# Distances between matrix inverse, stores and projection, and the split of the key norms, in a fused RWKV-7 and short-convolution block

## Chip, cores and metric

The kernel runs on one core of a Trainium2 chip. Time is the device time of one execution, in microseconds (us). The core has TensorE (PE, matmuls), VectorE (DVE), ScalarE (ACT), GpSimd (POOL) and SyncE (SP), which here issues DMA transfers. PSUM is the memory that PE writes to; SBUF holds everything else that is on the core.

## What is computed

A layer on 512 tokens with 16 learned tokens in front (528 positions, model width 2048): a norm, one wide projection, two groups of heads on its columns, one output projection added to the input, a final norm.

```python
hn = _rmsnorm(h_res, norm_in_g[l])
P = hn @ w_in[l]                      # 528 x 2048 @ 2048 x 8320
Pr, Pc = P[..., :RW_COLS], P[..., RW_COLS:]
...
# group A: RWKV-7, 16 heads of 64
def step(S, inp):
    r_t, w_t, k_t, v_t, kk_t, b_t = inp
    sa = jnp.einsum('bhvk,bhk->bhv', S, kk_t)
    S = (S * w_t[:, :, None, :]
         - sa[..., None] * b_t[:, :, None, :]
         + v_t[..., None] * k_t[:, :, None, :])
    y_t = jnp.einsum('bhvk,bhk->bhv', S, r_t)
    return S, y_t
...
kk = kk / jnp.maximum(jnp.linalg.norm(kk, axis=-1, keepdims=True), 1e-12)
y_a = (yn + bonus) * jax.nn.silu(g_r)
...
# group B: short convolution
y_b = Bg * _causal_depthwise_conv(Cg * hc, conv_w[l]) * jax.nn.silu(g_c)
mix = jnp.concatenate([y_a, y_b], axis=-1)
h_res = h_res + mix @ w_out[l]
```

The recurrence runs in 9 chunks of 64 positions. Within a chunk it needs the inverse of a triangular 64 x 64 matrix for each head, which is built from the products of all keys of the chunk with each other (the Gram matrix).

## The kernel before

**The projection** is the bulk of PE's work: 65 tiles of 128 output columns by all positions. Each weight and each input is split into a high and a low part, and three products are added up (L315): high weights on high input, high on low, low on high. A tile has four quarters of the depth with 24 matmuls each where the positions are in two PSUM halves (258 + 256, or 264 + 264 columns), or 12 where they are one bank of 512 (the tiles B and gc). In a tile with two halves, the halves alternate by depth, so the first half is complete 12 matmuls before the second. SP loads the weights two quarters at a time (L134, `prefetch`, three raw buffers); ACT casts the high part (wh, L126); the low part (wl, L127) is subtracted by DVE for even quarters and by POOL for odd ones. There are six buffers for each part.

The tiles come in a fixed list: low rank, then k, r, v of pairs 0 and 1, g of both, and C, h, B, gc of one convolution tile; then for pairs 2 and 3, 4 and 5, 6 and 7 likewise; then the last four convolution tiles. A "pair" i is two heads. When a tile is complete, L334 takes it out of PSUM (`hh` for tile h, `b` for B, `pr_g` for g), and the convolution (L401 u on POOL, L403 on ACT, L405 on DVE, L413 and L419 the gates) follows behind the tiles h and B; L420 stores its result (`mixd`).

**Other work between projection matmuls.** The projection is a generator. `fill(ns)` takes matmuls out of it, until their estimated cost comes to ns; the numbers stand in the table FW (L43 to 46). PE's order is thus written out by hand: a stage of other work, a fill, the next stage. The orders on DVE, ACT, POOL and SP are made by a list scheduler from priorities and the estimated times.

`later(ns, fn)` puts a transfer on a list with a due time on the projection's clock, ns ahead; `run_pending` issues those that are due, each behind the last weight load on SP's queue. `stash_later` is the same for stores into the scratch array `opd`, from which the recurrence later loads.

**`prepare(i)`**, for each pair: low rank parts, key scalings, the Gram blocks (L631, into `gt`), the key norms and a row sum zb (L655 to 667), copies of the norms to n2 (L670), the transposes bt. The norms are a matmul of 128 x 2 ones against the squares of the keys, in high and low parts; the first 512 positions went into a bank of their own, the last 64 beside the last Gram block. The inverse of the 16 x 16 blocks, y, runs on DVE alone (L706 to 739), in many small links. Stores: y to scratch and back in the layout of 64 x 64 blocks (xT, xo; L745, L746, L754).

**`invert(two)`** for two pairs widens 16 to 64: `fill(solve_first)` for the first two pairs or `fill(solve)` for the others, all pending transfers, then xn (L794, a transpose on DVE, of xT), t (L801, 64 small matmuls, half for each pair), copies ts, z (L815), a predicated copy, and one more level (L825 to 866). At its end stands `fill(out)`, or `fill(begin)` behind the last two pairs.

**`recur`** follows: it loads ct, the operands of a chunk of all pairs (L883, eight loads a chunk), and runs the nine chunks; rz (L902) is the first product of a chunk, zs and zy (L954, L958) come later in it. Then the mixing is split (L1028 to 1042), with `last` and `mix` fills in between, the rest of the projection, and the output projection (L1087).

Of the kernel before, what the change touches and what calls it, by code (L numbers as in the profile page):

```python
# [9 lines left out]
F32 = mybir.dt.float32  # L10
# [8 lines left out]
P = 128  # L19
DM = 2048  # L20
KT = DM // P
SEQ = 512
META = 16
L = SEQ + META
CH = 64
NCH = SEQ // CH + 1
LP = NCH * CH
# [11 lines left out]
O_AR, O_KK, O_BR, O_X, O_V, O_B, O_K = 0, 128, 256, 320, 384, 448, 512  # L39
# [1 line left out]


FW = dict(  # L43
    evac=34, start=1062, lora=2200, gram=8000, gram_b=13500, gram2=5500, misc=2000, v=2000, vt=1000, solve=22500, solve_first=26000,
    tr=3200, lev=3000, cp=4200, out=1500, begin=17000, p=2900, u=2900, s=5200, last=3700, mix=2600,
)


# [28 lines left out]
def hymba_kernel(ctx: ExitStack, tc: tile.TileContext, xt, xtok, w_in, w_out, pv, lup, cst, msk, gf, out):  # L77
    nc = tc.nc
    ctx.enter_context(tc.manual_schedule(engines={mybir.EngineType.PE}))
    cp = ctx.enter_context(tc.tile_pool(name="cp", bufs=1))  # L80
# [16 lines left out]
    def col(off, i=0):  # L97
        return pvt[:, off + i : off + i + 1]
# [56 lines left out]
    pz = ph1.enter_context(tc.tile_pool(name="pz", bufs=2, space=PSUM))  # L155
    pi = ph1.enter_context(tc.tile_pool(name="pi", bufs=1, space=PSUM))
# [5 lines left out]
    def tr(name, dt=F32):  # L162
        return cq.tile([P, LP], dt, tag="tr", name=name, bufs=5)
# [118 lines left out]
    for b in range(2):  # L282
# [5 lines left out]
        out=omm, in0=pvt[:, V_MU : V_MU + 33], scalar1=-1.0, scalar2=1.0, op0=ALU.mult, op1=ALU.add  # L288
    )
    for d, off in (  # L290
# [4 lines left out]
            out=d, in0=pvt[:, off : off + 8], scalar1=0.5, scalar2=None, op0=ALU.mult  # L295
        )
    nc.vector.tensor_scalar(
        out=hv[:, 4], in0=pvt[:, V_KA : V_KA + 8], scalar1=-0.5, scalar2=1.0, op0=ALU.mult, op1=ALU.add
# [183 lines left out]
    def later(ns, fn):  # L482
        pending.append((clock[0] + ns, fn))
        pending.sort(key=lambda e: e[0])
# [30 lines left out]
    def low_rank(i, j, up, w0, name, pad):  # L515
        t = tr(name)
        nc.gpsimd.memset(t[:, META:CH], pad)
        hi, lo = up
        for a, b in ((0, 272), (272, L)):
            z = pz.tile([P, b - a], F32, tag="tz", name=f"{name}_{a}")  # L520
            nc.tensor.matmul(z, hi[:, j], la[:, j, a:b], start=True, stop=False)
            nc.tensor.matmul(z, lo[:, j], la[:, j, a:b], start=False, stop=True)
            with tc.high_priority(offset=AHEAD):
                if a == 0:
                    nc.scalar.activation(t[:, 0:META], z[:, 0:META], AF.Tanh, bias=w0, scale=0.5)
                    nc.scalar.activation(t[:, CH : 5 * CH], z[:, META:272], AF.Tanh, bias=w0, scale=0.5)
                else:
                    nc.scalar.activation(t[:, 5 * CH : LP], z, AF.Tanh, bias=w0, scale=0.5)
            fill(FW["lora"])
        return t  # L530
# [5 lines left out]
    def c3(t):  # L536
        return t.rearrange("p (c s) -> p c s", s=CH)
# [28 lines left out]
    def stash(i, src, o, n, row=0, rows_n=P, c0=0, cn=NCH, step=1):  # L566
        nc.sync.dma_start(spot(i, row, rows_n, c0, cn, step, o, n), src)
# [6 lines left out]
    def stash_later(ns, *a):  # L574
        later(ns, lambda: stash(*a))

    def prepare(i):
        p = i % 2
# [8 lines left out]
        tz = low_rank(i, 0, up, hv[:, 0, i : i + 1], f"tz{i}", -1.0)  # L587
# [12 lines left out]
            out=bk[:, :, 0], in0=c3(k), scalar=hv[:, 2, i : i + 1], in1=c3(te), op0=ALU.mult, op1=ALU.mult  # L600
# [3 lines left out]
            out=ta, in0=ta, scalar1=hv[:, 3, i : i + 1], scalar2=hv[:, 4, i : i + 1], op0=ALU.mult, op1=ALU.add  # L604
        )
        nc.vector.scalar_tensor_tensor(
            out=ar[:, :, 0], in0=c3(k), scalar=col(V_KK, i), in1=e1[:, :, 0:CH], op0=ALU.mult, op1=ALU.mult
# [8 lines left out]
            out=ar[:, 1:NCH, 1], in0=c3(r), in1=e1[:, 1:NCH, 1 : CH + 1], op=ALU.mult  # L616
        )
        nc.vector.scalar_tensor_tensor(
            out=r, in0=r, scalar=hv[:, 5, i : i + 1], in1=ta[:, CH:LP], op0=ALU.mult, op1=ALU.mult
# [8 lines left out]
        gt = cq.tile([P, 2, NCH, P], F32, tag=f"gt{p}", name=f"gt{i}")  # L628
        def gram(z, c, c0):
            for h, hs, ho in heads:  # L630
                nc.tensor.matmul(  # L631
                    z[h][:, c - c0],
                    bk[hs, c, h : h + 2, :].rearrange("p a s -> p (a s)"),
                    ar[hs, c].rearrange("p a s -> p (a s)"),
                    start=True, stop=True,
                )
# [17 lines left out]
        masked(zc, 4, 8)  # L654
        fill(FW["gram2"])  # L655

        ze = [pz.tile([P, P + CH], F32, tag="tz", name=f"g{i}_8_{h}") for h in range(2)]
        gram([z[:, 0:P].unsqueeze(1) for z in ze], 8, 8)
        n2 = tr(f"n2{i}")
        zn = pi.tile([2, SEQ], F32, tag="misc", name=f"n2_{i}")  # L660
        zs = ((zn, 0, SEQ), (ze[0][0:2, P : P + CH], SEQ, LP))
        for z, a, b in zs:
            nc.tensor.matmul(z, ones[:, P : P + 2], sqh[:, a:b], start=True, stop=False)
            nc.tensor.matmul(z, ones[:, P : P + 2], sql[:, a:b], start=False, stop=True)
# [11 lines left out]
        bt = cq.tile([P, NCH - 1, 2, CH // 2, 2], F32, tag="bt", name=f"bt{i}")  # L676
# [5 lines left out]
        sx = scr_x[i % 2]  # L682
# [4 lines left out]
        def blocks(t):  # L687
            return bass.AP(tensor=t.tensor, offset=t.offset, ap=[[BLK, 8 * NCH], [CH, 16], [1, 16]])
# [7 lines left out]
        d = cq.tile([NB, 256], F32, tag="d", name=f"d{i}").rearrange("p (s t) -> p s t", t=16)  # L696
        stash_later(1500, i, ar.rearrange("p c a s -> p c (a s)"), O_AR, 2 * CH)
        for h, hs, ho in heads:
            stash_later(2500 + 1000 * h, i, gt[ho, h], O_KK, 2 * CH, 64 * h, 64)
            stash_later(4500 + 1000 * h, i, gt[hs, h, :, CH:P], O_BR, CH, 64 * h, 64)  # L700
        nd = cq.tile([NB, 16], F32, tag="nd", name=f"nd{i}")
        behind(d, blocks(sg))
        behind(nd, sn.rearrange("(p s) -> p s", s=16))
        y = cq.tile([NB, 256], F32, tag="y", name=f"y{i}").rearrange("p (s t) -> p s t", t=16)
# [14 lines left out]
        for m in (2, 4, 8):  # L719
            for b in range(16 // (2 * m)):  # L720
# [4 lines left out]
                    out=pq,  # L725
# [5 lines left out]
                    out=tq.rearrange("p (i j) -> p i j", i=m), in_=pq, op=ALU.add, axis=AX.X  # L731
                )
                nc.vector.tensor_tensor(
                    out=pq,
# [16 lines left out]
                    ),  # L751
                )

        later(20500 if p else 29000, lambda: nc.sync.dma_start(blocks(sx), y))  # L754
        later(22500 if p else 33000, load_inverse)

        for h, hs, ho in heads:
            for b in range(2):
                for t in range(2):
                    stash_later(  # L760
                        6500 + 1000 * (4 * h + 2 * b + t), i, bt[64 * h + 32 * b : 64 * h + 32 * b + 32, :, t].rearrange("p c s a -> p c (s a)"),
                        O_B + 64 * b, 64, 64 * h + 32 * t, 32, 0, NCH - 1,
                    )
        until("v", i)
        v = got["v", i]
# [244 lines left out]
    for i in range(0, NPAIR, 2):  # L1010
        invert([prepare(i), prepare(i + 1)])
# [56 lines left out]
    last = [[pw.tile([P, 512], F32R, name=f"wlast{a}{j}") for j in range(NL)] for a in range(2)]  # L1068
# [82 lines left out]
    for n in range(4):  # L1151
# [5 lines left out]
        for jj in range(first):  # L1157
# [3 lines left out]
            if n < 2 and jj % 4 == 2:  # L1161
                t, cols = jj // 4, slice(0, 512) if n == 0 else slice(512, DM)
# [11 lines left out]
    with tc.manual_schedule(engines={mybir.EngineType.DVE, mybir.EngineType.Activation, mybir.EngineType.Pool}):  # L1174
# [9 lines left out]
        for part in range(2):  # L1184
# [3 lines left out]
            if part == 0:  # L1188
                finish(2)
                nc.vector.tensor_tensor(  # L1190
                    out=fv[:, 3, 0:1], in0=fv[:, 3, 0:1], in1=ssq[:, 3, 3:4], op=ALU.add
# [60 lines left out]
```

## Time and profile before

| | us |
|---|---|
| median of three runs | 1051.81 |
| lowest and highest | 1050.89, 1053.62 |
| the profiled execution | 1051.02 |
| its span, first to last instruction | 1049.2 |
| mean granted clock of PE | 0.994 |
| DMA moved | 167.48 MB, mean 160 GB/s |

In a row of the timeline the numbers are the start, the duration and, in brackets at the end, how long the engine had been idle and what ended that. `x4` means four instructions put together in a row. In the list of waits the three numbers behind the colon are the total, how many, and the longest. "128x512" is partitions by elements. "issue" is time for which the profile shows no cause. PE's durations overlap, since matmuls are pipelined.

### The profile page before, as it was taken

The numbers are of one execution on the slowest core, as the hardware profiler recorded it, in microseconds if no ns is written. First come the engines' busy times: TensorE is split into PE (matmuls) and PEld (weight loads), VectorE is DVE, ScalarE is ACT, GpSimd is POOL, SyncE is SP. The second block draws the span as 40 slices with busy tenths as digits, with TensorE's granted clock in tenths as the row PEclk, the third lists the DMA queues.
The fourth block names the chain that finished last, engine by engine and source line by source line (L and its number), as shares of the span: only waits on it lengthen the run. The fifth ranks groups of instructions, "written<-read, shape, count | busy, mean of one in ns | idle before, by whom it ended". The sixth has DMA issues, their size and how long they took to land.

```text
span 1049.2 us, 23744 instructions
## 1 busy us (share of the span) xinstructions
PE 1031.6 (98%) x9845; PEld 940.8 (90%) x9845; DVE 580.1 (55%) x1088; ACT 360.0 (34%) x666; POOL 311.1 (30%) x315
## 2 busy tenths in 40 slices
PE   8999998999999999999999999999999999999996
PEld 6999996999998999989999988889898988888885
DVE  6786855569754669753768752444555761212222
ACT  7554313433322434332443232222233342323232
POOL 0132613323222323222323131223233232424132
PEclk8999999999999999999999999999999999999998
DMA  8436565464763273853374748777654958323314
GB/s 292 141 101 166 128 160 145 114 159 103 193 182 114 82 193 84 202 159 114 104 171 103 196 144 291 241 219 221 211 135 150 286 182 296 101 86 95 101 61 161
DMA packets 183404, 167.48 MB, mean 160 GB/s; under 512 B 121472, under 2 KB 143744, under 8 KB 182912
## 3 DMA queue, kind: packets, MB, share of 16 engines
q1 hardware_dynamic: 182720, 164.90, 54.6%
q8 instruction: 77, 1.26, 0.5%
q10 hardware_dynamic: 576, 1.07, 0.3%
q14 instruction: 31, 0.25, 0.1%
HBM read 129.05 MB, written 36.88 MB: 158 GB/s over the span
## 4 chain that ended last, share of the span: by engine, by line
PE 94%; DMA 2%; issue 1%; DVE 1%; POOL 0%; SPq 0%; ACT 0%; DVEq 0%; ACTq 0%; POOLq 0%
PE o L1087 17%; PE ps_v L315 9%; PE ps_g L315 9%; PE ps_k L315 9%; PE ps_gc L315 9%; PE ps_r L315 8%; PE ps_B L315 8%; PE ps_C L315 8%; PE ps_h L315 8%; PE g L631 2%; DMA wq<-in_w_in_dram 1%; PE zs L954 1%; PE zy L958 1%; PE ps_lora L315 1%; PE rz L902 1%
## 5 line engine op out<-in xcount | busy, mean ns | idle before, releaser
L127 POOL TENSOR_TENSOR wl<-wr,wh 128x512 fp32r<-128x512 f32 x150 | 208.8, 1392 | 460.0 <-ACT wh L126 439.6
L126 ACT CAST wh<-wr 128x512 fp32r<-128x512 f32 x312 | 190.0, 618 | 411.7 <-PE o L1087 93.0
L127 DVE TENSOR_TENSOR wl<-wr,wh 128x512 fp32r<-128x512 f32 x162 | 121.7, 756 | 224.4 <-ACT wh L126 223.2
L1087 PE MATMUL o<-wh,m 128*128 128x512 f32 (+1 forms) x484 | 145.2, 384 | 0.0
L1087 PEld LDWEIGHTS o<-wh,m 128*128 128x128 f32 x484 | 89.6, 188 | 21.3
L1087 PE MATMUL o<-wl,m 128*128 128x512 f32 (+1 forms) x242 | 92.6, 389 | 0.0
L315 PE MATMUL ps_h<-xh,wh 128*128 128x258 f32 (+1 forms) x256 | 72.7, 284 | 0.6 <-issue 0.6
L315 PE MATMUL ps_k<-xh,wh 128*128 128x264 f32 x256 | 73.2, 286 | 0.0
L315 PE MATMUL ps_v<-xh,wh 128*128 128x264 f32 x256 | 73.2, 286 | 0.0
L315 PE MATMUL ps_k<-xl,wh 128*128 128x264 f32 x256 | 73.1, 285 | 0.0
L315 PE MATMUL ps_k<-xh,wl 128*128 128x264 f32 x256 | 72.9, 285 | 0.0
L315 PE MATMUL ps_r<-xh,wh 128*128 128x258 f32 (+1 forms) x256 | 72.2, 282 | 0.7 <-ACT wh L225 0.7
L315 PE MATMUL ps_v<-xh,wl 128*128 128x264 f32 x256 | 72.7, 284 | 0.0
L315 PE MATMUL ps_v<-xl,wh 128*128 128x264 f32 x256 | 72.7, 284 | 0.0
L315 PE MATMUL ps_C<-xh,wh 128*128 128x258 f32 (+1 forms) x256 | 72.5, 283 | 0.0
L315 PE MATMUL ps_g<-xl,wh 128*128 128x258 f32 (+1 forms) x256 | 72.4, 283 | 0.0
L315 PE MATMUL ps_h<-xl,wh 128*128 128x258 f32 (+1 forms) x256 | 72.3, 283 | 0.0
L315 PE MATMUL ps_C<-xl,wh 128*128 128x258 f32 (+1 forms) x256 | 72.3, 282 | 0.0
L315 PE MATMUL ps_r<-xh,wl 128*128 128x258 f32 (+1 forms) x256 | 72.1, 282 | 0.0
L315 PE MATMUL ps_r<-xl,wh 128*128 128x258 f32 (+1 forms) x256 | 72.0, 281 | 0.0
L315 PE MATMUL ps_g<-xh,wh 128*128 128x258 f32 (+1 forms) x256 | 71.9, 281 | 0.0
L315 PE MATMUL ps_C<-xh,wl 128*128 128x258 f32 (+1 forms) x256 | 71.9, 281 | 0.0
(274 smaller groups left out, 2715.9 us busy)
## 6 DMA issues: line engine op xcount, KB each, us to landing
wr<-in_w_in_dram SPq DMA_DIRECT2D x127, 512.0 KB
ct<-opd SPq DMA_DIRECT2D x64, 288.0 KB
wr<-in_w_out_dram SPq DMA_DIRECT2D x32, 512.0 KB
opd<-ar SPq DMA_DIRECT2D x8, 576.0 KB
opd<-gt SPq DMA_DIRECT2D x16, 288.0 KB
opd<-bt SPq DMA_DIRECT2D x64, 64.0 KB
xres<-in_xtok_dram SPq DMA_DIRECT2D x4, 768.0 KB
out_dram<-xres SPq DMA_DIRECT2D x6, 512.0 KB
```

The source lines that it names most:

```text
L126: nc.scalar.copy(hi, rq)
L127: eng.tensor_tensor(out=lo, in0=rq, in1=hi.bitcast(F32), op=ALU.subtract)
L315: nc.tensor.matmul(ps[r], ww[:, w], xx[:, kt, a:b], start=(kt == 0 and n == 0), stop=(kt == KT - 1 and n == 2))
L631: nc.tensor.matmul(z[h][:, c - c0], bk[hs, c, h : h + 2, :].rearrange("p a s -> p (a s)"), ar[hs, c].rearrange("p a s -> p (a s)"), start= ...
L902: nc.tensor.matmul(z[e][ho if e else hs, 0, k], t[hs, o : o + CH], t[hs, O_V : O_V + CH] if part else st[hs, 4 * e + k], start=(part == 0 ...
L954: nc.tensor.matmul(d[hs, j], w, x[hs], start=(a == 0), stop=(a == b - 1))
L958: nc.tensor.matmul(d[ho, j], t[hs, o : o + CH], x[hs], start=(a == 0), stop=(a == b - 1))
L1087: nc.tensor.matmul(ps[t + p], mm[:, tk], ww[:, o], start=(jj == 0 and q == 0), stop=(jj == KT - 1 and q == 2))
```

## The change

Three things, all in the table and in `prepare`. The fills in front of the inverses grow: solve from 22500 to 24500, solve_first from 26000 to 30000, and begin, between the last inverse and the recurrence, from 17000 to 19500. The key norms are taken in two parts of 288 positions instead of 512 and 64; the second still lies beside the last Gram block, whose tile becomes wider for the first head and narrower for the second. And due times move: the Gram blocks' stores by 3000 ns each, bt's eight stores from 6500 + 1000 n to 9000 + 900 n, and, for pair 1 alone, the store of y and the load of xT and xo by 2000 ns.

```diff
 FW = dict(
-    evac=34, start=1062, lora=2200, gram=8000, gram_b=13500, gram2=5500, misc=2000, v=2000, vt=1000, solve=22500, solve_first=26000,
-    tr=3200, lev=3000, cp=4200, out=1500, begin=17000, p=2900, u=2900, s=5200, last=3700, mix=2600,
+    evac=34, start=1062, lora=2200, gram=8000, gram_b=13500, gram2=5500, misc=2000, v=2000, vt=1000, solve=24500, solve_first=30000,
+    tr=3200, lev=3000, cp=4200, out=1500, begin=19500, p=2900, u=2900, s=5200, last=3700, mix=2600,
 )
...
-        ze = [pz.tile([P, P + CH], F32, tag="tz", name=f"g{i}_8_{h}") for h in range(2)]
+        ze = [pz.tile([P, P + 288 * (1 - h)], F32, tag="tz", name=f"g{i}_8_{h}") for h in range(2)]
         gram([z[:, 0:P].unsqueeze(1) for z in ze], 8, 8)
         n2 = tr(f"n2{i}")
-        zn = pi.tile([2, SEQ], F32, tag="misc", name=f"n2_{i}")
-        zs = ((zn, 0, SEQ), (ze[0][0:2, P : P + CH], SEQ, LP))
+        zn = pi.tile([2, 288], F32, tag="misc", name=f"n2_{i}")
+        zs = ((zn, 0, 288), (ze[0][0:2, P : P + 288], 288, LP))
         for z, a, b in zs:
             nc.tensor.matmul(z, ones[:, P : P + 2], sqh[:, a:b], start=True, stop=False)
             nc.tensor.matmul(z, ones[:, P : P + 2], sql[:, a:b], start=False, stop=True)
...
         for h, hs, ho in heads:
-            stash_later(2500 + 1000 * h, i, gt[ho, h], O_KK, 2 * CH, 64 * h, 64)
-            stash_later(4500 + 1000 * h, i, gt[hs, h, :, CH:P], O_BR, CH, 64 * h, 64)
+            stash_later(5500 + 1000 * h, i, gt[ho, h], O_KK, 2 * CH, 64 * h, 64)
+            stash_later(7500 + 1000 * h, i, gt[hs, h, :, CH:P], O_BR, CH, 64 * h, 64)
...
-        later(20500 if p else 29000, lambda: nc.sync.dma_start(blocks(sx), y))
-        later(22500 if p else 33000, load_inverse)
+        later((22500 if i == 1 else 20500) if p else 29000, lambda: nc.sync.dma_start(blocks(sx), y))
+        later((24500 if i == 1 else 22500) if p else 33000, load_inverse)
...
-                        6500 + 1000 * (4 * h + 2 * b + t), i, bt[64 * h + 32 * b : 64 * h + 32 * b + 32, :, t].rearrange("p c s a -> p c (s a)"),
+                        9000 + 900 * (4 * h + 2 * b + t), i, bt[64 * h + 32 * b : 64 * h + 32 * b + 32, :, t].rearrange("p c s a -> p c (s a)"),
```

## The prediction

> **What bounds the kernel now.** I read the page's busy line and its chain of work first, then the list of what PE waited for, then windows and timelines around each wait.
>
> ```profile
> PE 1031.6 (98%) x9845; PEld 940.8 (90%) x9845; DVE 580.1 (55%) x1088; ACT 360.0 (34%) x666; POOL 311.1 (30%) x315
> ...
> PE 94%; DMA 2%; issue 1%; DVE 1%; POOL 0%; SPq 0%; ACT 0%; DVEq 0%; ACTq 0%; POOLq 0%
> ...
> PE ps_B L315 <- DVE wl L127: 1.6, 1, 1.6
> ...
> PE ps_gc L315 <- DVE wl L127: 0.9, 1, 0.9
> PE ps_h L315 <- issue: 0.6, 1, 0.6
> PE t L801 <- DVE xn L794: 0.5, 1, 0.5
> PE rz L902 <- DMA ct<-opd: 0.5, 1, 0.5
> PE zy L958 <- issue: 0.2, 1, 0.2
> ...
> 791.90:861.80 69.90, 69.90 (x407) 61.47 (x406) 46.75 (x63) 25.81 (x44) 24.67 (x18) 1.00 0.72 215
> ```
>
> TensorE (PE) is busy 98% of the span and carries 94% of the chain, so time can change in two ways only: matmuls that become cheaper or dearer, and moments at which PE stands still. Behind the arrow is what ended a wait, then total, number, longest (us). The six rows are all the waits inside the body: 1.6+0.9+0.6+0.5+0.5+0.2 = 4.3 us. The rest of PE's idle time lies in the first 22 us and the last 10, which the change doesn't touch. A change that does not shorten matmuls can win 4.3 us at most (0.4%), while what it can lose is open. The last row (window, PE busy and count, the other engines, clock, DMA share, GB/s) is the stretch of pure projection behind the recurrence: from here the generator takes what the kernel wants earlier.
>
> **Part 1: key norms in two halves.**
>
> ```profile
> 84.52 0.40 PE L663 MATMUL n<-sq_h,ones 128*2 128x512 f32 x1
> ...
> 84.98 0.19 PE L663 MATMUL g<-sq_h,ones 128*2 128x64 f32 x1
> ...
> 85.04 0.48 PE L666 MATMUL zb<-rk_h,ones 128*128 128x512 f32 x1
> 85.36 0.40 PE L667 MATMUL zb<-rk_l,ones 128*128 128x512 f32 x1
> 85.59 0.28 PE L315 MATMUL ps_r<-xl,wh 128*128 128x258 f32 x1
> ...
> 302.77 0.28 PE L315 MATMUL ps_h<-xl,wh 128*128 128x256 f32 x1
> ...
> 303.59 0.28 PE L315 MATMUL ps_h<-xh,wl 128*128 128x256 f32 x1
> ```
>
> The first columns are start and duration; durations overlap in the pipeline, so a matmul costs the distance to the next start. From 84.52 to 85.59 the group takes 1.07 us: 2 x 0.23 for 512 columns, 0.06 for the two of 64, and then 0.32 + 0.23 for zb. The first zb costs 0.09 more than its kind: its 128-column weights don't disappear behind a 64-column matmul. A 256-column one costs (303.59 - 302.77)/7 = 0.117, so 288 columns cost 0.117 + (32/256) x (0.23 - 0.117) = 0.131 (estimate). After: 4 x 0.131 + 2 x 0.23 = 0.99, so 0.08 less, times 8 groups = 0.7 us. Bounds: 0 (the 0.09 stays) and 0.8. The two copies to n2 change from 512 + 64 columns to 288 + 288, the same sum, on ACT, which is busy 34%.
>
> **Part 2: the first inverse (solve_first 26000 to 30000).** Three of the six waits stand here.
>
> ```profile
> 150.82 0.43 DVE L334 TENSOR_TENSOR hh<-ps_h,rs 128x258 f32<-128x258 f32 x1 [3.09 <-PE ps_h L315]
> ...
> 153.09 0.41 DVE L334 TENSOR_TENSOR hh<-ps_h,rs 128x256 f32<-128x256 f32 x1
> 153.42 1.16 DVE L733 TENSOR_TENSOR prod<-y,tt 72x512 f32<-72x512 f32 x1
> ...
> 157.67 1.54 POOL L127 TENSOR_TENSOR wl<-wr,wh 128x512 fp32r<-128x512 f32 x1 [1.92 <-ACT wh L126]
> ...
> 158.00 1.76 DVE L127 TENSOR_TENSOR wl<-wr,wh 128x512 fp32r<-128x512 f32 x1
> ...
> 159.81 0.50 PE L315 MATMUL ps_B<-xh,wl 128*128 128x512 f32 x1 [1.59 <-DVE wl L127]
> ...
> 168.12 0.70 DVE L794 STREAM_TRANSPOSE xn<-xT 128x512 f32<-128x512 f32 x1
> ...
> 168.88 0.69 PE L801 MATMUL t<-xn,gt 64*64 64x64 f32 x32 [0.50 <-DVE xn L794]
> ```
>
> DVE works in program order. At 150.82 it had stood 3.09 us before the first half of hh, with the last links of the 16x16 inverse (L739, L724, L730, L733) queued behind it. All but L733 and the last L739 then run in front of the second half at 153.09, and from there leads a chain: u on POOL, the convolution on ACT and DVE, wl at 158.00, PE at 159.81. In the changed program's order L739, L724 and L730 come ahead of the first hh, in that 3.09 us hole; only L733 (1.16 us at 153.42) is left between the halves. The second half then waits for its own matmuls: its last is 12 matmuls (12 x 0.117 = 1.4) behind that of the first half (150.82 - 0.32 + 1.4 = 151.9), so it runs at about 152.2 instead of 153.09. The chain moves up by 0.9, and the 1.59 shrinks to about 0.7.
>
> The wait at 168.88 goes: L801 comes 18 matmuls of 512 columns later (18 x 0.23 = 4.1 us) with xn behind a load that moves about 1 us only (one weight load now stands ahead of the stored y on SP's queue). The 0.92 of ps_gc stays: the product b still stands on DVE ahead of the split it waits for. Gain 0.9 + 0.5 = 1.4 us; bounds 0 and 1.59 + 0.92 + 0.50 = 3.0.
>
> The Trainium skill ("SBUF — State Buffer", section "Who interferes with whom") says that a DVE instruction with two inputs in SBUF contends with a GpSimd instruction that reads SBUF, and that who issues first decides who waits. The trace agrees: wl at 158.00 took 1.76 us, until just after POOL's wl ended at 157.67 + 1.54 = 159.21. By that rule the ps_B wait would go altogether (0.7 us more gain) if DVE's split were issued first; both follow ACT's casts, which move together, so I keep POOL first.
>
> **Part 3: the later inverses (solve 22500 to 24500), three pairs.** None of them waits today.
>
> ```profile
> 282.98 0.43 DVE L334 TENSOR_TENSOR pr_g<-ps_g,rs 128x258 f32<-128x258 f32 x1 [2.14 <-PE ps_g L315]
> 283.33 0.15 DVE L733 TENSOR_TENSOR prod<-y,tt 72x8 f32<-72x8 f32 x1
> ...
> 298.92 0.63 SPq L746 DMA_DIRECT2D xo<-sx  x1
> ...
> 302.23 0.69 DVE L127 TENSOR_TENSOR wl<-wr,wh 128x512 fp32r<-128x512 f32 x1 [4.01 <-ACT wh L126]
> 302.84 0.70 DVE L794 STREAM_TRANSPOSE xn<-xT 128x512 f32<-128x512 f32 x1
> ...
> 303.80 1.16 PE L801 MATMUL t<-xn,gt 64*64 64x64 f32 x64
> 304.89 0.39 PE L315 MATMUL ps_h<-xh,wh 128*128 128x256 f32 x1
> ...
> 308.07 0.28 PE L315 MATMUL ps_h<-xh,wl 128*128 128x256 f32 x1
> ...
> 308.39 0.42 DVE L334 TENSOR_TENSOR hh<-ps_h,rs 128x256 f32<-128x256 f32 x1 [0.74 <-PE ps_h L315]
> ```
>
> L801 moves 18 matmuls back within the h tile, and so passes the end of the tile's first half: that half's last matmul is the 15th behind the old place of t, and t now comes three later. The scheduler answers on DVE: the evacuation hh of that half, which stood behind xn, now stands in front of wl and of the xn of the pair's second member. Before, DVE's order was wl 302.23, xn 302.84 and hh after t. Now xn cannot start before PE has finished a matmul that is only three ahead of the one that needs xn.
>
> By rows: that 15th matmul starts at 303.59 + 15 x 0.117 = 305.35 (t no longer in between). An hh follows the start of its last matmul by about 0.32 (308.39 after 308.07), so 305.67. To the next instruction 0.35 (282.98 to 283.33), wl to xn 0.61, xn 0.70: it ends at 307.33, PE goes on at 307.39 (0.06 as at 168.82 to 168.88). PE would want t's second half at 303.59 + 18 x 0.117 + 0.21 + 0.47 = 306.4 (0.21 is the step into t, 0.5 its first half, of the 1.09 from 303.80 to 304.89). Lost: 1.0 us per pair. The orders of pairs 4/5 and 6/7 show the same, so 3.0 us. Lower bound 0.6 each (hh at once), upper 2.2 (restart 0.1, and a wl drawn out as at 158.00, 1.1): 1.8 to 6.5. I take 3.0, the value that the rows of this place give without either extra.
>
> The stall delays nothing but PE. The loads behind it: y's chain of the second member, whose first links ran ahead of pr_g at 282.98, now starts behind it; as DVE stood idle for 2.14 us there, it ends about 2 us later; the last of its four loads is issued at some 301 instead of 298.92 and, with the 3.9 us at most that the load took before (298.92 to 302.84), is in by 304.9, ahead of 306.6.
>
> **Part 4: begin 17000 to 19500, and the stores.**
>
> ```profile
> 632.55 2.92 SPq L883 DMA_DIRECT2D ct<-opd  x6
> 639.08 0.32 SPq L420 DMA_DIRECT2D mixd<-cv  x1
> 639.50 5.64 SPq L883 DMA_DIRECT2D ct<-opd  x10
> ...
> 644.78 0.33 PE L902 MATMUL rz<-ct 64*64 64x64 f32 x4 [0.48 <-DMA ct<-opd]
> ...
> 632.00:636.00 4.00, 4.00 (x20) 3.30 (x19) 0.81 (x2) 0.92 (x2) 0.14 (x1) 1.00 0.68 171
> 636.00:640.00 4.00, 4.00 (x36) 4.00 (x35) 2.94 (x4) 1.58 (x3) 1.30 (x1) 1.00 1.01 382
> ```
>
> The recurrence's first rz comes 41 matmuls later (2000 + 2500 ns of projection; 41 x 0.117 = 4.8 us): at 649.1 instead of 644.3 for its last four. On SP, the store of the convolution at 639.08 used to stand between the sixth and seventh of the eight loads ct; now it stands in front of seven of them. 256 KB and 7 x 288 KB at 382 KB/us take 5.9 us. After the issue at 632.55 the window to 636 carried under half of the next one's 382 GB/s, so data flow some 2 to 3 us after the issue: 639.1 + 3 + 5.9 = 648.0. So the 0.48 wait goes; bounds a gain of 0.5 and a loss of 0.6 (begin's own delay not sufficient by one load, 0.75). I take 0.4. The moved stores of Gram blocks and bt are the same transfers at the same size, some 3 us of projection later; what reads them is this recurrence, after 632. Their issues on SP cost nothing while SP keeps ahead of the weight loads. The projection taken earlier, 4 + 3 x 2 + 2.5 = 12.5 us, is missing from the 69.9 us of pure projection at 791.9. The mixing steps there spread over 4 x 3.7 + 8 x 2.6 = 35.6, and 57.4 remain: cost nothing; without that cover the mixing would add what is missing.
>
> **Sum.** -0.7 - 1.4 - 0.4 + 3.0 = +0.5 us on the profiled execution's 1051.0: 1051.5. The median of the three runs, 1051.8, lies 0.8 above the profiled one, so 1052.3 in the median's terms.
>
> **The rivals.** A measurement can tell 0.3% (3.2 us) from no change: under 1048.7 is faster, over 1055.0 slower.
>
> *Faster: hh doesn't hold xn.* If the hh waits in pairs 1 to 3 cost nothing, 2.5 us of gains remain: 1049.3. If the other rows of the first pair (0.7 of ps_B, 0.92 of ps_gc) and the issue rows (0.6, 0.2) go too, 1046.9. For it: the shift in the first pair also moves every weight split after it, so any of these can vanish. Against it: DVE's order is fixed in the program, and 150.82 shows DVE standing 3.09 us for such an hh with ready work behind.
>
> *Slower: the xT loads come late.* In pairs 1 to 3 the y chain ends about 2 us later while the store of y and the loads keep their place on the projection's clock. If SP stands at the store and the loads land after 306.6 instead of 304.9, each us beyond adds 1 us per pair. It decides beyond 1.7 us of delay; at 2.7 us it makes 3 us, 1055.3, at 3.7 us 1058. For it: SP is one queue, on which the store of y holds up all that follows. Against it: before, 3.9 us was the whole way from issue to use.
>
> *No effect.* Positions move, but waits move along with them, as splits are ordered by the same projection clock: only the norms' 0.7 us: 1051.1.
>
> **How the numbers follow.** Forecast 0.40 (its own range 1050.5 to 1054.5), faster 0.24, slower 0.26, no effect 0.10. Of the faster case some three quarters lie below 1048.7 (0.18), of the slower one most above 1055.0, and a little of the forecast's upper bound (6.5 us lost) too: 0.27. The rest, 0.55, is within. Leaving out a tenth at each end gives 1047.8 to 1056.5.
>
> **What would show it.** Right: a list of PE's waits with three new rows t from xn of about 1.0 us each, near 306, 457 and 608, each with an hh directly ahead of wl and xn on DVE; the t row of the first pair gone; ps_B's 1.6 down to about 0.7; the norm group 0.99 long with four 288-column matmuls; rz's row gone. Wrong: no t rows (then faster), a t row ended by xT's load or over 2 us long (then slower), a wait on weight splits that is new, or PE's busy sum changed by more than 1 us.

## The result, and the profile after

| | before | changed |
|---|---|---|
| median of 22 runs each, us | 1051.82 | 1050.01 |
| lowest to highest | 1048.86 to 1053.90 | 1047.15 to 1051.71 |
| profiled execution, its span | 1051.02, 1049.2 | 1049.89, 1048.1 |

The ratio is 0.9982, with a 95% interval of 0.9975 to 0.9989: 1.8 us faster, between 1.2 and 2.6. The forecast was 1052.3, slower by half a us. The time lies within the wide range of 1047.8 to 1056.5 and within the 0.3% called no change, but below the forecast's own range of 1050.5 to 1054.5, and the sign was wrong.

The busy line of the page and PE's waits in the changed kernel (line, what ended the wait, then total, number, longest in us):

```profile
PE 1030.6 (98%) x9845; PEld 940.2 (90%) x9845; DVE 577.1 (55%) x1088; ACT 359.7 (34%) x666; POOL 302.2 (29%) x315
```

```profile
PE t L801 <- DVE xn L794: 2.3, 3, 0.8
...
PE ps_gc L315 <- DVE wl L127: 0.9, 1, 0.9
...
PE rz L902 <- DMA ct<-opd: 0.6, 2, 0.4
...
PE ps_h L315 <- issue: 0.3, 1, 0.3
PE rz L954 <- issue: 0.3, 1, 0.3
```

The three new waits of t are there, the old one is gone, ps_gc is the same to a tenth. ps_B is gone altogether, where 0.7 was forecast; rz is still there. PE's busy time is 1.0 us less with the same 9845 matmuls.

The first norm group in PE's timeline of the changed kernel (start, duration, instruction):

```profile
84.03 0.29 PE L663 MATMUL n<-sq_h,ones 128*2 128x288 f32 x1
84.16 0.29 PE L664 MATMUL n<-sq_l,ones 128*2 128x288 f32 x1
84.29 0.30 PE L663 MATMUL g<-sq_h,ones 128*2 128x288 f32 x1
84.42 0.30 PE L664 MATMUL g<-sq_l,ones 128*2 128x288 f32 x1
84.55 0.39 PE L666 MATMUL zb<-rk_h,ones 128*128 128x512 f32 x1
84.78 0.40 PE L667 MATMUL zb<-rk_l,ones 128*128 128x512 f32 x1
85.02 0.28 PE L315 MATMUL ps_r<-xl,wh 128*128 128x258 f32 x1
```

84.03 to 85.02 is 0.99 us, as worked out, with 0.13 for 288 columns and 0.23 for the first zb instead of 0.32. The load of its weights now starts 0.13 us before it (84.42); in the kernel before it started 0.03 before (85.01), behind a 64-column matmul.

DVE's timeline in the first pair, and POOL's at the same place:

```profile
150.14 0.43 DVE L334 TENSOR_TENSOR hh<-ps_h,rs 128x258 f32<-128x258 f32 x1 [1.19 <-PE ps_h L315]
150.48 1.14 DVE L733 TENSOR_TENSOR prod<-y,tt 72x512 f32<-72x512 f32 x1
151.54 0.42 DVE L334 TENSOR_TENSOR hh<-ps_h,rs 128x256 f32<-128x256 f32 x1
151.88 0.67 DVE L739 TENSOR_REDUCE y<-prod 72x64 f32<-72x512 f32 x1
...
155.58 1.79 DVE L127 TENSOR_TENSOR wl<-wr,wh 128x512 fp32r<-128x512 f32 x1
```

```profile
152.04 1.29 POOL L401 TENSOR_TENSOR u<-u,hh 128x514 f32<-128x514 f32 x1 [9.90 <-DVE hh L334]
```

From the first hh to the second are 1.40 us instead of 2.27. And u on POOL takes 1.29 us where it took 2.17, as POOL's row of the kernel before shows:

```profile
153.58 2.17 POOL L401 TENSOR_TENSOR u<-u,hh 128x514 f32<-128x514 f32 x1 [10.80 <-DVE hh L334]
```

There u began just after the start of DVE's L733 (153.42 to 154.58), which reads two tiles in SBUF, and ended 1.17 us after that; here L733 is issued before the second hh and u begins behind both. Of the other seven u of the kernel before, six take 1.28 to 1.31 us. The one at 797.84 took 1.76, beside DVE's L994 (796.66 to 798.42, also with two inputs in SBUF), and ended 1.18 us after that. L739, which reads one tile and runs beside u here (151.88), doesn't lengthen it.

PE and DVE around t in pair 3:

```profile
302.58 0.69 PE L801 MATMUL t<-xn,gt 64*64 64x64 f32 x32
304.04 0.70 PE L801 MATMUL t<-xn,gt 64*64 64x64 f32 x32 [0.76 <-DVE xn L794]
304.66 0.39 PE L315 MATMUL ps_h<-xh,wh 128*128 128x256 f32 x1
```

```profile
302.34 0.43 DVE L334 TENSOR_TENSOR hh<-ps_h,rs 128x258 f32<-128x258 f32 x1 [6.47 <-PE ps_h L315]
302.68 0.68 DVE L127 TENSOR_TENSOR wl<-wr,wh 128x512 fp32r<-128x512 f32 x1
303.28 0.70 DVE L794 STREAM_TRANSPOSE xn<-xT 128x512 f32<-128x512 f32 x1
```

DVE stands idle for 6.47 us until the end of the h half, then hh, wl and xn follow in one chain, and PE goes on 0.06 after xn ends. The rows in the other two places, at 455.85 and 607.66, are the same: 0.76 each. It is the step of part 3, in the order it gave.

SP's queue ahead of the recurrence, and what PE waits for there:

```profile
631.70 0.44 SPq L883 DMA_DIRECT2D ct<-opd  x1
638.19 0.33 SPq L420 DMA_DIRECT2D mixd<-cv  x1
638.62 10.41 SPq L883 DMA_DIRECT2D ct<-opd  x15
```

```profile
648.00 0.33 PE L902 MATMUL rz<-ct 64*64 64x64 f32 x4 [0.17 <-DMA ct<-opd]
648.74 0.33 PE L902 MATMUL rz<-ct 64*64 64x64 f32 x4 [0.41 <-DMA ct<-opd]
```

Seven loads stand behind the store, as foreseen, and PE goes on from the last that rz waits for 10.5 us after the store's issue, where 8.9 was worked out.

**A stretch to compare by.** Executions differ ahead of everything that the change touches. So I take, for the kernels below, the stretch from the first norm matmul (L663) to the first matmul of the output projection (L1087), each read from the list of a line's instructions (after the colon the least, median and greatest ns, then first and last start):

```profile
L663 PE MATMUL n<-sq_h,ones x8: 291/295/295, 84.0 to 569.6; 128*2 128x288 f32 x8
...
L1087 PE MATMUL o<-wh,m x484: 278/393/402, 860.5 to 1023.0; 128*128 128x512 f32 x148, 128*128 128x256 f32 x14
```

That is 776.5 us. Before it is 861.6 - 84.5 = 777.1.

### The profile page after: what moved, and what is told of

It reads as the page before. It is cut to its first block, busy times and chain, and to the rows that moved or that the text cites. A ratio compares the mean times of both kernels' runs of the same rounds, so it can differ in the third digit from the quotient of the medians.

```text
span 1048.1 us, 23743 instructions
## 1 busy us (share of the span) xinstructions
PE 1030.6 (98%) x9845; PEld 940.2 (90%) x9845; DVE 577.1 (55%) x1088; ACT 359.7 (34%) x666; POOL 302.2 (29%) x315
## 4 chain that ended last, share of the span: by engine, by line
PE 92%; DMA 4%; DVE 2%; SPq 1%; issue 1%; ACT 0%; POOL 0%; DVEq 0%; ACTq 0%
PE o L1087 17%; PE ps_v L315 9%; PE ps_gc L315 9%; PE ps_k L315 9%; PE ps_g L315 9%; PE ps_r L315 8%; PE ps_B L315 8%; PE ps_C L315 7%; PE ps_h L315 7%; PE g L631 2%; PE zs L954 1%; PE ps_lora L315 1%; PE zy L958 1%; DMA gated<-g 1%; PE rz L902 1%; DVE wl L127 1%
## 5 line engine op out<-in xcount | busy, mean ns | idle before, releaser
L127 POOL TENSOR_TENSOR wl<-wr,wh 128x512 fp32r<-128x512 f32 x150 | 204.4, 1363 | 466.0 <-ACT wh L126 450.4
L1087 PE MATMUL o<-wh,m 128*128 128x512 f32 (+1 forms) x484 | 145.4, 384 | 0.0
L1087 PEld LDWEIGHTS o<-wh,m 128*128 128x128 f32 x484 | 89.6, 188 | 21.3
L1087 PE MATMUL o<-wl,m 128*128 128x512 f32 (+1 forms) x242 | 92.7, 390 | 0.0
L315 PE MATMUL ps_h<-xh,wl 128*128 128x258 f32 (+1 forms) x256 | 72.3, 282 | 0.0
```

The lines of the kernel that those rows point to most:

```text
L127: eng.tensor_tensor(out=lo, in0=rq, in1=hi.bitcast(F32), op=ALU.subtract)
L315: nc.tensor.matmul(ps[r], ww[:, w], xx[:, kt, a:b], start=(kt == 0 and n == 0), stop=(kt == KT - 1 and n == 2))
L1087: nc.tensor.matmul(ps[t + p], mm[:, tk], ww[:, o], start=(jj == 0 and q == 0), stop=(jj == KT - 1 and q == 2))
```

## The experiments

Ratios are to the kernel before, run beside each, with 95% intervals. "Stretch" is the one above, in one profile of each.

| kernel | median, us | ratio | stretch | ps_B | t from xn | rz from ct |
|---|---|---|---|---|---|---|
| before, again | 1051.93 | 1.0002 (0.9990 to 1.0014) | 777.8 | 1.6 | 0.5 | 1.2 |
| changed, again | 1049.52 | 0.9983 (0.9974 to 0.9992) | 776.2 | none | 3 x 0.76 | 0.4 |
| norms alone | 1050.01 | 0.9985 (0.9974 to 0.9995) | 776.5 | 0.6 | 0.5 | 1.0 |
| stores alone | 1052.18 | 1.0007 (0.9995 to 1.0020) | 778.0 | 1.6 | 0.8 | 0.7 |
| norms and stores | 1049.29 | 0.9985 (0.9972 to 0.9997) | 774.9 | none | 0.5 | 0.7 |
| solve_first and pair 1's due times | 1050.00 | 0.9991 (0.9982 to 1.0001) | 776.3 | 1.6 | none | 0.9 |
| begin alone | 1049.76 | 0.9986 (0.9977 to 0.9994) | 776.1 | 1.6 | 0.5 | none |
| solve alone | 1054.84 | 1.0028 (1.0016 to 1.0040) | 780.7 | 1.6 | 2.8 | 0.8 |
| changed, solve 22500 | 1046.86 | 0.9955 (0.9942 to 0.9967) | 773.1 | none | none | none |
| changed, solve 24000 | 1047.01 | 0.9952 (0.9938 to 0.9965) | 773.1 | none | none | none |
| changed, solve 25500 | 1073.88 | 1.0207 (1.0192 to 1.0221) | 798.6 | none | 17.6 | none |

A shorter stretch, from the first norm matmul to the one of the third pair's group, holds only the first of the inverses (84.52 to 223.91 before, 84.03 to 220.75 with the change). It repeats to 0.05 us between two profiles of one kernel, so it can tell the parts apart:

| kernel | first to third norm group, us | against before |
|---|---|---|
| before, twice | 139.39, 139.41 | |
| stores alone | 139.38 | 0.0 |
| solve_first and pair 1's due times | 138.67 | -0.7 |
| norms alone | 138.24 | -1.2 |
| norms and stores | 137.55 | -1.85 |
| changed, twice | 136.72, 136.77 | -2.65 |

**Both kernels again.** No edit.

> The kernel before, unchanged, for a second profile. The waits theory (what the change does is the sum of PE's waits and the norms' matmuls, the same in every execution): the waits ps_B from wl about 1.6, ps_gc 0.9, t from xn 0.5 stand again, within 0.1 us; time equal to before. Rival (waits vary between executions, and the first profile of before showed fewer than usual): some wait in the body is longer by 0.5 us or more, or one is new.

> The changed kernel, unchanged, for a second profile. Waits theory: three waits of t from xn of 0.76 us each, ps_gc 0.9, no ps_B, as in its first profile; about 1.8 us under before. Rival (waits vary): these differ by 0.3 us or more from the first profile, above all rz from ct, which ends with a load.

Waits that end with DVE are the same to a tenth from one execution to the next. The one that ends with a load is not: rz waited 0.48 and 1.20 us before, 0.58 and 0.41 with the change. So the 0.5 which the prediction started from was the low one of two. The first norm matmul started at 84.5 and 84.3, and 84.0 and 85.7: an execution's time scatters by over a us from the start alone.

**The norms alone.**

```diff
-zn = pi.tile([2, SEQ], F32, tag="misc", name=f"n2_{i}")
-zs = ((zn, 0, SEQ), (ze[0][0:2, P : P + CH], SEQ, LP))
+zn = pi.tile([2, 288], F32, tag="misc", name=f"n2_{i}")
+zs = ((zn, 0, 288), (ze[0][0:2, P : P + 288], 288, LP))
```

> The key norms' part alone: 288 + 288. By the prediction's part 1: 0.7 us of matmuls, 1051.1, and the waits of before. Theory of a reordered DVE: the shorter norm group alone makes the scheduler put the last links of the 16x16 inverse ahead of the first hh, so u on POOL runs 1.3 instead of 2.2 us and the ps_B wait falls from 1.6 to between 0 and 0.6, though solve_first is as before: 1049.9 to 1050.5. t from xn stays at 0.5.

DVE and POOL of this kernel in the first pair:

```profile
150.33 0.43 DVE L334 TENSOR_TENSOR hh<-ps_h,rs 128x258 f32<-128x258 f32 x1 [1.47 <-PE ps_h L315]
150.67 1.14 DVE L733 TENSOR_TENSOR prod<-y,tt 72x512 f32<-72x512 f32 x1
151.85 0.68 DVE L739 TENSOR_REDUCE y<-prod 72x64 f32<-72x512 f32 x1
152.45 0.41 DVE L334 TENSOR_TENSOR hh<-ps_h,rs 128x256 f32<-128x256 f32 x1
```

```profile
152.94 1.30 POOL L401 TENSOR_TENSOR u<-u,hh 128x514 f32<-128x514 f32 x1 [10.64 <-DVE hh L334]
```

Without any longer fill, links of the 16x16 inverse have moved ahead of hh. Between the two hh it is still 2.12 us, nearly the 2.27 of before; but u runs in 1.30 instead of 2.17. The 0.15 and the 0.87 are the 1.0 that ps_B lost of its 1.6 us. An edit of four matmuls on PE and the two copies behind them, in groups of which the first stands at 84 us, changed the list scheduler's order on DVE at 150. Which of these pieces it reacted to is not shown.

**The stores, and the norms with the stores.**

```diff
-stash_later(2500 + 1000 * h, ...)
-stash_later(4500 + 1000 * h, ...)
+stash_later(5500 + 1000 * h, ...)
+stash_later(7500 + 1000 * h, ...)
...
-6500 + 1000 * (4 * h + 2 * b + t)
+9000 + 900 * (4 * h + 2 * b + t)
```

> The later due times of the Gram blocks' and bt's stores alone. By the prediction's part 4 they cost and bring nothing: the time of before, ps_B 1.6, ps_gc 0.9, t from xn 0.5. Rival (the stores make room for the loads that rz waits for, or for weights): a wait in the body shrinks by 0.5 us or more, and the time by as much.

> Norms 288 + 288 and the later stores, no fill changed. Theory that the gain at ps_B is DVE's order alone: here the order is hh, L733, hh, L739 as in the changed kernel (with the norms alone L739 also stands ahead of the second hh, and 0.6 of the 1.6 us was left), so ps_B goes to 0 without any longer fill; ps_gc 0.9 and t from xn 0.5 stay. 1.6 + 0.1 restart + 0.65 of matmuls = 2.3 us under before. Rival (solve_first takes the last 0.6): ps_B about 0.6, 1.7 us under before.

The later stores alone change nothing in the first inverse, and the ratio can't be told from 1. They have one small cost: at 303.43 DVE's xn waits 1.22 us for the load of xT, and t 0.30 behind it, which is the second wait in the 0.8 of the table. Together with the norms they move one more instruction: L739 goes behind the second hh, and ps_B is gone without solve_first. The waits of that kernel:

```profile
PE ps_gc L315 <- DVE wl L127: 0.9, 1, 0.9
...
PE rz L902 <- DMA ct<-opd: 0.7, 2, 0.4
PE ps_h L315 <- issue: 0.6, 1, 0.6
PE t L801 <- DVE xn L794: 0.5, 1, 0.5
```

The stretch fell by 2.5 us against the mean of the two before (777.45), near the 2.3 expected; the ratio, 1.6 us with an interval from 0.3 to 2.9, agrees and doesn't tell it from the rival's 1.7. What does is that ps_B's row is gone, and the 0.7 us between the norms' 138.24 and 137.55 in the shorter stretch.

**solve_first.**

```diff
-solve_first=26000
+solve_first=30000
...
-later(20500 if p else 29000, ...)
-later(22500 if p else 33000, load_inverse)
+later((22500 if i == 1 else 20500) if p else 29000, ...)
+later((24500 if i == 1 else 22500) if p else 33000, load_inverse)
```

> solve_first 30000 alone, with pair 1's store and load 2000 ns later; the norms stay 512 + 64. By the prediction's part 2 (the longer fill moves the chain of the 16x16 inverse): ps_B falls from 1.6 to about 0.7 and t from xn goes, 1.4 us gained. Theory that the norms' edit reordered DVE: here DVE's order around hh is that of before, so ps_B stays at 1.6, and only t from xn (0.5 and 0.1 for the restart) goes: about 0.6 us gained.

```profile
PE ps_B L315 <- DVE wl L127: 1.6, 1, 1.6
...
PE ps_gc L315 <- DVE wl L127: 0.9, 1, 0.9
PE rz L902 <- DMA ct<-opd: 0.9, 2, 0.5
```

ps_B stays whole, and the t row is gone. The interval of the ratio reaches 1; the shorter stretch is 0.7 us less. So the longer first fill is worth the 0.5 us of xn and a restart, and nothing of the rest that the prediction put under its name.

**begin.**

```diff
-begin=17000
+begin=19500
```

> begin 19500 alone. By the prediction's part 4 the wait of rz from ct (0.5 and 1.2 us in two profiles of before) shrinks, by 0.4 us or more; the other waits stay. Rival (the store of the convolution holds the loads back as far as rz moves): rz waits 0.5 or more still.

rz does not wait any more, and the kernel is 1.5 us faster (0.6 to 2.4). Here, as before, six loads stand ahead of the store of the convolution; in the changed kernel it is one (the SP rows above), and rz waits in both its profiles. With the change and solve at 22500 or 24000 it is six and three, and rz doesn't wait. That fits a gain of begin which is partly given back by the order on SP; no kernel here moves that store alone.

**solve: alone, taken back, and at two other lengths.**

```diff
-solve=22500
+solve=24500     # alone, in the kernel before
...
-solve=24500     # in the changed kernel
+solve=22500     # and 24000, and 25500
```

> solve 24500 alone. Theory of hh in front of xn: three waits t from xn of 0.76 us, each with a restart of 0.1: 2.6 us more than before, about 1054.4, with the waits of before beside them. Rival (the longer solve gains by giving the loads time): 1051.8 or less.

> The changed kernel with solve back at 22500, all else as changed. Theory that the longer solve costs by hh in front of xn: the three waits of t from xn (0.76 each and 0.1 for each restart) go, all else stays as in the changed kernel: 2.6 us less, about 1047.4, under both kernels. Rival (the longer solve is what brought the gain): time back to about 1051.

> The changed kernel with solve at 24000 instead of 24500: t moves by about 5 matmuls less, and on DVE xn of the second member stands in front of hh again. Theory of hh in front of xn: what costs is the place on DVE, not the length, so the three waits are gone and the time is that of solve 22500, 1046.9. Rival (the wait grows with the length of the fill): three quarters of the cost remain, 0.57 per pair, about 1049.

> The changed kernel with solve at 25500: now both halves of hh and the convolution's first DVE instruction (L405) stand in front of xn on DVE. Theory of hh in front of xn: xn waits behind hh, u on POOL (1.3), ACT (0.7) and L405 (1.0), about 4.2 us per pair, so 12.6 us over solve 22500: about 1059.5. Rival (the wait was loads that come late, and a longer fill gives them time): t waits less than 0.76, at most 1050.

Alone, the longer solve costs 2.9 us (1.7 to 4.2), and taken out of the changed kernel it gives 3.2 us by the medians (2.7 against the changed kernel run beside it) and 3.2 by the stretch. At 24000 nothing is lost: DVE of that kernel has xn ahead of hh again.

```profile
302.35 0.71 DVE L794 STREAM_TRANSPOSE xn<-xT 128x512 f32<-128x512 f32 x1 [1.13 <-DMA xT<-sx]
304.83 0.43 DVE L334 TENSOR_TENSOR hh<-ps_h,rs 128x258 f32<-128x258 f32 x1 [1.77 <-PE ps_h L315]
```

So it isn't the length: 1500 ns more cost nothing, and 2000 cost three us, since between them t passes the end of the h half. At 25500 both hh, and the convolution's DVE step that waits for POOL and ACT, stand ahead of xn; DVE's rows and PE's:

```profile
302.62 0.43 DVE L334 TENSOR_TENSOR hh<-ps_h,rs 128x258 f32<-128x258 f32 x1 [6.47 <-PE ps_h L315]
304.02 0.42 DVE L334 TENSOR_TENSOR hh<-ps_h,rs 128x256 f32<-128x256 f32 x1 [0.97 <-PE ps_h L315]
306.58 1.54 DVE L405 SCALAR_TENSOR_TENSOR cv<-u,pvt,cv 128x512 f32<-128x512 f32 x2 [2.13 <-ACT cv L403]
308.04 1.75 DVE L127 TENSOR_TENSOR wl<-wr,wh 128x512 fp32r<-128x512 f32 x1
309.71 0.70 DVE L794 STREAM_TRANSPOSE xn<-xT 128x512 f32<-128x512 f32 x1
```

```profile
310.47 1.13 PE L801 MATMUL t<-xn,gt 64*64 64x64 f32 x32 [5.85 <-DVE xn L794]
311.53 0.79 PE L315 MATMUL ps_B<-xh,wh 128*128 128x512 f32 x1
312.12 0.63 PE L315 MATMUL ps_B<-xl,wh 128*128 128x512 f32 x1
312.55 0.63 PE L315 MATMUL ps_B<-xh,wl 128*128 128x512 f32 x1
```

The chain is the one expected, hh, u, L403, L405, wl, xn. PE waits 5.85 us for it instead of 4.2: both of the convolution's DVE steps run (1.54 for two, not 1.0 for one) and wl takes 1.75. The wait is not all that it costs: PE's clock falls, in the last column but two of the windows:

```profile
310.00:316.00 6.00, 5.53 (x43) 4.46 (x44) 1.10 (x2) 2.11 (x4) 1.27 (x1) 0.51 0.31 90
316.00:330.00 14.00, 14.00 (x181) 11.05 (x180) 6.69 (x13) 4.22 (x9) 4.01 (x5) 1.00 0.33 97
```

After the 5.85 us of idleness PE runs at 0.51 until about 316, with matmuls of 512 columns 0.43 us apart instead of 0.23. What that costs shows from the first matmul of tile h to the last of gc, the same 450 matmuls in each kernel. In the three places this takes 46.29, 45.23 and 46.15 us, against 38.75, 38.75 and 38.76 in the changed kernel (and 37.83 or 37.84 with solve 24000). Of the 7.5, 6.5 and 7.4 us more, 5.1 each are the longer wait; 2.4, 1.4 and 2.3 are left for the slow clock. These 21.4 us are most of the 22.2 by which the stretch grew; the medians differ by 23.9, and the rest is not accounted for.

The Trainium skill ("TensorE: Matmul & The Clock Gate", section "What's actually happening") says that an idle window of about 3.4 us halves the clock. The runs agree on both sides of it: 5.85 us did, 1.59 us did not, as the window around it in the kernel before shows:

```profile
150.00:170.00 20.00, 16.98 (x139) 13.38 (x138) 11.16 (x14) 4.33 (x8) 7.72 (x6) 1.00 0.36 84
```

In windows of 0.1 us the granted clock falls at 309.1, 466.1 and 626.5 and is back at 315.9, 472.9 and 633.4, each time 6.8 us later. All six lie whole multiples of 3.413 us apart, 95 of them from the first to the last. Of the 6.8 us, 5.4, 3.1 and 5.2 lie behind the end of the wait, so what a wait costs beyond itself depends on where it falls: in the second place the clock fell 2.1 us after PE's last matmul, and least of the slow time was left.

## Why the prediction was wrong, by its own steps

Part 1, the matmuls of the norms: right, 0.07 to 0.09 us in each of eight groups, and a little more around them (with the norms alone, the two groups from the third to the fifth take 150.85 us instead of 151.06, so 0.8 in all). What it left out is what the edit does away from PE. It counted instructions and asked what covers them, but not what a shorter PE stage does to the orders on the other engines.

Part 2 is where the number failed. It read the new DVE order rightly (L739, L724 and L730 ahead of the first hh) and put the chain 0.9 us earlier. But it took u on POOL at its old 2.17 us and only moved it. u had been that long because it ran beside L733, and with L733 out of the way it took 1.29 (2.16 or 2.17 in all six profiles with the old order on DVE, 1.29 or 1.30 in the seven with L733 ahead of the second hh): 0.9 earlier, and 0.9 shorter, more than the 1.59 that was there. The Trainium skill ("SBUF — State Buffer", section "Who interferes with whom") says that a DVE instruction with two inputs in SBUF contends with a GpSimd instruction that reads SBUF. The trace agrees for u: 2.17 us beside L733 and 1.29 without. The prediction weighed this for wl and not for u, which its rows leave out. So the term "0.9 + 0.5 = 1.4" should have been 1.59 + 0.50 and the restarts: 2.45 us, as the shorter stretch has it (139.4 - 136.75, less 0.2 for the norms of two groups). The part also named the wrong edit: the runs show the reordering to come from the norms (1.0 of the 1.6) and the stores beside them (the rest), and solve_first to bring xn alone.

Part 3 was right, place and price: 1.0 a pair forecast, 0.76 of idleness and about 0.15 for the restart measured (two such waits lengthen the way from the first norm group to the eighth by 1.8 us in the changed kernel over that with solve 22500: 569.6 - 84.0 = 485.6 against 483.8). Its forecast that the loads of xT would still be in time held: no t of the changed kernel waits for them. They are not far from mattering: at 24000 xn does wait for xT, 1.13 us, in DVE's time and not in PE's, and with the stores alone PE lost 0.30 us to them.

Part 4 said that rz's wait goes, gain 0.4. It didn't go, as the loads took 10.5 us and not 8.9; what made them longer stays open. The gain of 0.3 to 0.4 on the mean of two profiles is the difference to a wait that was larger than the one profile of before had it (0.84 against 0.48).

With these sizes the sum is -0.8 - 2.45 - 0.35 + 2.75 = -0.85 instead of +0.5. The stretch fell by 1.1 on the mean of two profiles each; the further 0.25 is of the size by which the rows that end with "issue" fell (0.8 and 0.5 in the profiles of before, 0.6 and none in those of the changed kernel), whose cause no view shows. The medians say 1.8, at least 1.2; what lies between stays open, as executions scatter by more than that.

Of the rivals, "faster: hh doesn't hold xn" was wrong in its cause, as hh did hold xn; but its aside that further waits of the first pair could vanish was what happened. "Slower: the xT loads come late" did not occur in the changed kernel. "No effect" fell too: waits did not move along with the positions, they vanished or appeared. The bound of 4.3 us plus the norms' 0.7 was a good one: the best kernels, with the three t rows out, gained 4.7 and 5.0 us by their ratios and 4.35 by the stretch, though ps_gc's 0.9 still stands in them.

The better kernel is the changed one with solve at 22500 or 24000: 1046.86 and 1047.01 us, 0.45% and 0.48% under before (0.33 to 0.62), and 0.3% under the change as it was made.

## What to carry to other kernels

Before putting more work ahead of a stage, ask which results of that work another engine picks up, and whether that pick-up now stands in front of what the stage needs in the other engine's order. 1500 ns were free here, 2000 cost 3 us, 3000 cost 27. And where a scheduler orders the other engines, a small edit can reorder them: cost the new order with the durations that instructions have without their old neighbours, and run each part of a change alone before a gain is credited to it. Compare short stretches between two fixed instructions: the one here repeated to 0.05 us, where whole executions scattered by several.

## What was not expected of the hardware

A POOL instruction took 2.17 us beside a DVE instruction with two inputs in SBUF and 1.29 without it, and this 0.88 was about half of what ps_B had to lose. A wait of 5.85 us cost 1.4 to 2.4 us more in slow clock, by where it fell among steps of 3.41 us. And two matmuls of 64 columns are not free: a weight load of 128 columns showed 0.09 us behind them, and none behind one of 288.
